# A two-block layer stack on one core: first operands in smaller pieces on two queues, attention states in turn, shifted weight rows in 14 more groups, another last root

## The chip, the cores and the metric

The kernel runs on one core of one Trainium2 chip. The metric is the device time in microseconds; lower is better. The time before is the median of three runs.

## The reference, cut to what matters

All values are float32, one sequence of 256 rows of 1024 (`x`) and 256 memory rows (`mem`). The first block mixes three branches and ends with a feed-forward layer:

```python
h = rms_norm(x, norm_mix)
z = h @ w_in                                   # rnn, q, k, v, g, decay, mq, gates
out_a = rg_lru(causal_dwconv(z_rnn, ...), ...) # linear recurrence over the rows
o_gla = chunked_gla(z_q, z_k, z_v, log_alpha)  # 4 heads, chunks of 64 rows:
#   state = decay * state + k_end.T @ v, one state per chunk and head
out_b = rms_norm(o_gla, gla_norm) * silu(z_g)
mk, mv = split(rms_norm(mem, mem_norm) @ w_mem_kv)
out_c = softmax(mq @ mk.T * scale) @ mv        # 4 heads
x = x + sum(sigmoid(z_gate) * proj(out_a, out_b, out_c)) @ w_out
h2 = rms_norm(x, norm_ffn)
x = x + (gelu(gate) * val) @ w_down            # of causal_dwconv(h2 @ w_up)
x = rms_norm(x, final_norm)
```

The second block has 6 attention heads, a state-space mixer and a pooling mixer side by side, then a SiLU feed-forward layer, and ends with

```python
x = x + (silu(gate) * up) @ w_down_2
return rms_norm(x, norm_final_2)
```

## The kernel before, in words

**Products.** Every long product is made of three matmuls (`mm3`, lines L203 to L205): both operands are split into a high and a low part in a 32-bit format that TensorE reads in one pass, and high x high, high x low and low x high are added in PSUM. `split` (L154) makes the parts: ScalarE copies the high part (L156, or L159 with a gain), VectorE subtracts for the low part (L157, L160). Weights arrive in groups (`memk0`, `v2`, `gate2_0`, `gu5`, ...), each one DMA on SP's queue into a `raw` tile of 1 MB. `emit_half` (L169) splits half a group at a time into a `wh` and a `wl` tile; `load_w` keeps three halves ahead of the half that is used. `chunk_T` (L207) multiplies a group so that features lie on partitions, with the weights as stationary operand and 256 columns; `chunk_tok` (L231) so that rows lie on partitions, with the activations stationary and the weights moving. A half of a usual group is four slices of 256 columns, 24 matmuls. `PLACE` (L73) shifts the `wh` and `wl` tiles of three groups (`up3`, `xbc3`, `gu6`): half 0 begins 28 floats, half 1 begins 30 floats into its buffer.

**Order.** The groups come in the order of `wplan` (L88): `memk`, `memv`, `mq`, `zrnn`, `qk`, `rga`, `rgx`, `v`, `g`, then for the branches 2, 0, 1 four pairs of `gate` and `br`, then `wout`; `up` with `dn` between; the second block's `vz`, `qk2`, `xbc`, `pool`; `wo2`; `gu` with `dn2`. Smaller work (scores, states, transposes, sums) runs on two lanes of generators; `step()` (L404) runs one piece of each lane after a group. `gla_state` (L707) has one piece for each of three chunk states: for the four heads a matmul of 64 rows (L720), rows 0 to 63 for an even chunk and 64 to 127 for an odd one. `gla_scores` comes one step before it, `gla_out` after it, in four further steps, two of them with small products and one with transposes. At each such step TensorE leaves the long products for the small ones; these places are called joints here.

**Start.** ScalarE's queue loads 16 columns of gains (L253). SP's queue loads in turn two memory slices (256 KB, L344) and a quarter of `memk0` and of `memk1` (256 KB each, L363), four times. Thirteen warm-up matmuls (L258) run until then. The sums of squares of the memory rows (`Ssq`, L282 to L297) come after these products; `memk2` follows.

**End.** The last two down products leave 4 banks, two for each half of the rows. For each half (L1333 on) ScalarE squares and sums two banks, VectorE adds, ScalarE takes the root, VectorE takes its reciprocal with one Newton step (L1344 to L1347), and the banks are scaled by it and by the gains `nfb` (`scaled`, L1331). For the second half of the rows the first bank is multiplied by the gains early (L1339) and scaled by ScalarE (L1354); the second bank is scaled by VectorE in two pieces. Tile, the layer that orders the instructions of each engine and makes their waits, may move an instruction within its engine's order.

## Time and profile before

| | |
|---|---|
| median of three runs | 797.58 us (796.61 to 798.03) |
| the profiled execution | 797.59 us, of which span 795.8 us |
| TensorE, busy share of the span | 99% |
| VectorE, ScalarE | 75%, 61% |
| DMA read and written | 141.20 MB, 1.05 MB |
| instructions | 15612 |

The span runs from the first to the last instruction of the program; the rest of the profiled execution's time lies around it. An engine's busy time counts each stretch once in which it has an instruction under way. A matmul record is longer than the distance to the next one, since matmuls are pipelined; so the pace of a stretch is read from the starts, not from the durations. A matmul of two full 32-bit operands leaves two records.

### The profile page before, as it was taken

The page shows a single profiled execution, that of the slowest core. Times are in us where ns is not written, and L with a number is a line of the kernel's source. Part 1 is how long each engine was busy: PE and PEld are TensorE (multiplying, and loading weights), DVE is VectorE, ACT ScalarE, POOL GpSimd, SP SyncE. Part 2 cuts the span into 40 slices and gives each one's busy share as a digit, 9 for nine tenths or more (in the row PEclk, how much of TensorE's full clock was granted, in tenths as well). Part 3 has the DMA queues.
Part 4 walks back from the last instruction along what each step waited for, and adds up shares of the span by engine and source line. Part 5 has one row for each costly group of instructions (what it writes and reads, how often), then busy time and mean ns, then how long its engine had stood idle before and what let it go on. Part 6 is the DMA issues. An engine that isn't in the chain of part 4 may idle for free.

```text
span 795.8 us, 15612 instructions
## 1 busy us (share of the span) xinstructions
PE 785.1 (99%) x6460; PEld 760.9 (96%) x6460; DVE 598.6 (75%) x980; ACT 481.8 (61%) x770; POOL 10.2 (1%) x23
## 2 busy tenths in 40 slices
PE   8999999999999999999999999999999999999996
PEld 8999989999889999999999999999899999999995
DVE  6988757965667777898778887899898756656663
ACT  6845679964345555666556565768976544444443
POOL 0000110000000000000000000000000000000000
PEclk9999999999999999999999999999999999999999
DMA  8864544364445665366555555263174544555521
GB/s 281 305 229 152 175 133 176 114 231 140 144 142 201 203 213 204 110 243 228 171 203 207 173 204 198 103 257 113 49 268 157 215 181 167 203 200 180 205 106 53
DMA packets 23526, 144.03 MB, mean 181 GB/s; under 512 B 2896, under 2 KB 3424, under 8 KB 8480
## 3 DMA queue, kind: packets, MB, share of 16 engines
q1 hardware_dynamic: 22464, 140.98, 49.9%
q0 software_dynamic: 704, 1.80, 0.6%
q8 instruction: 50, 0.82, 0.4%
q10 hardware_dynamic: 288, 0.27, 0.1%
q14 instruction: 20, 0.16, 0.1%
HBM read 141.20 MB, written 1.05 MB: 179 GB/s over the span
## 4 chain that ended last, share of the span: by engine, by line
PE 91%; DVE 4%; ACT 3%; issue 1%; DMA 1%; DVEq 0%; SPq 0%; ACTq 0%
PE ps L203 23%; PE ps L204 22%; PE ps L205 22%; PE aux L203 6%; PE aux L205 6%; PE aux L204 5%; DVE wl L157 2%; PE aux L521 1%; PE ps L220 1%; PE ps L227 1%; PE ps L218 1%; DMA raw<-w 1%; ACT wh L156 1%; PE aux L720 1%; ACT L1154 0%
## 5 line engine op out<-in xcount | busy, mean ns | idle before, releaser
L157 DVE TENSOR_TENSOR wl<-raw,wh 128x1024 fp32r<-128x1024 f32 (+4 forms) x276 | 322.1, 1172 | 119.5 <-ACT wh L156 117.7
L156 ACT ACTIVATE wh<-raw 128x1024 fp32r<-128x1024 f32 (+4 forms) x276 | 277.9, 1015 | 207.2 <-PE ps L204 159.6
L203 PE MATMUL ps<-H,wh 128*128 128x256 f32 x1320 | 368.2, 279 | 1.2 <-ACT wh L156 1.2
L205 PE MATMUL ps<-H,wl 128*128 128x256 f32 x1320 | 366.3, 278 | 0.2 <-DVE wl L157 0.2
L204 PE MATMUL ps<-H,wh 128*128 128x256 f32 x1320 | 366.3, 278 | 0.0
L203 PEld LDWEIGHTS ps<-H,wh 128*128 128x128 f32 x1320 | 248.0, 188 | 3.5 <-issue 1.8
L204 PEld LDWEIGHTS ps<-H,wh 128*128 128x128 f32 x1320 | 248.7, 188 | 0.3
L205 PEld LDWEIGHTS ps<-H,wl 128*128 128x128 f32 x1320 | 248.1, 188 | 0.4 <-DVE wl L157 0.4
L203 PE MATMUL ps<-wh,H 128*128 128x256 f32 (+2 forms) x192 | 54.6, 285 | 0.0
L204 PE MATMUL ps<-wl,H 128*128 128x256 f32 (+2 forms) x192 | 54.0, 281 | 0.3 <-DVE wl L157 0.3
L205 PE MATMUL ps<-wh,H 128*128 128x256 f32 (+2 forms) x192 | 54.1, 282 | 0.0
L205 PE MATMUL aux<-S,wl 128*128 128x256 f32 x192 | 53.1, 277 | 0.0
L204 PE MATMUL aux<-S,wh 128*128 128x256 f32 x192 | 53.1, 276 | 0.0
L203 PE MATMUL aux<-S,wh 128*128 128x256 f32 x192 | 53.1, 276 | 0.0
L156 ACT ACTIVATE S<-t 128x256 fp32r<-128x256 f32 x46 | 19.0, 415 | 50.3 <-DVE t L921 26.5
L543 DVE SCALAR_TENSOR_TENSOR t<-t,par,t 128x255 f32<-128x255 f32 (+1 forms) x96 | 40.1, 478 | 0.1
L204 PEld LDWEIGHTS ps<-wl,H 128*128 128x128 f32 x192 | 36.1, 188 | 0.5 <-DVE wl L157 0.5
L203 PEld LDWEIGHTS ps<-wh,H 128*128 128x128 f32 x192 | 36.1, 188 | 0.4 <-issue 0.4
L205 PEld LDWEIGHTS ps<-wh,H 128*128 128x128 f32 x192 | 36.1, 188 | 0.0
L205 PEld LDWEIGHTS aux<-S,wl 128*128 128x128 f32 x192 | 36.1, 188 | 0.0
L203 PEld LDWEIGHTS aux<-S,wh 128*128 128x128 f32 x192 | 36.1, 188 | 0.0
L204 PEld LDWEIGHTS aux<-S,wh 128*128 128x128 f32 x192 | 36.1, 188 | 0.0
(327 smaller groups left out, 1070.8 us busy)
## 6 DMA issues: line engine op xcount, KB each, us to landing
raw<-w SPq DMA_DIRECT2D x115, 1024.0 KB, 4.8
raw<-w SPq DMA_DIRECT2D x12, 768.0 KB, 4.3
raw<-w SPq DMA_DIRECT2D x12, 256.0 KB, 5.3
raw<-w SPq DMA_DIRECT2D x2, 896.0 KB, 4.5
raw<-w SPq DMA_DIRECT2D x1, 1088.0 KB, 6.2
raw<-w SPq DMA_DIRECT2D x1, 1048.0 KB, 4.8
R<-memT SPq DMA_DIRECT2D x4, 256.0 KB, 5.5
R<-xT SPq DMA_DIRECT2D x2, 512.0 KB, 8.8
```

The source lines that it names most:

```text
L156: act.activation(dst_h, src, AF.Copy)
L157: dve.tensor_tensor(dst_l, src, dst_h.bitcast(F32), op=ALU.subtract)
L203: pe.matmul(o, lh, rh, start=start, stop=False, skip_group_check=skip)
L204: pe.matmul(o, lh, rl, start=False, stop=False, skip_group_check=skip)
L205: pe.matmul(o, ll, rh, start=False, stop=stop, skip_group_check=skip)
L218: pe.matmul(ps[:, m, :], wh[:, k, c], x[0][:, kk, :], start=kk == 0 and m == 0, stop=False, skip_group_check=True)
L220: pe.matmul(ps[:, m, :], wl[:, k, c], x[0][:, kk, :], start=False, stop=False, skip_group_check=True)
L227: pe.matmul(ps[:, m, :], wh[:, k, m * P:(m + 1) * P], x[1][:, kk, :], start=False, stop=kk == nk - 1, skip_group_check=True)
L521: pe.matmul(ps[r0:r1, :], mv[:, mt, hd * DV + d0:hd * DV + d0 + r1 - r0], pts[hd][:, mt, :], start=mt == 0, stop=mt == 1, skip_group_check ...
L543: dve.scalar_tensor_tensor(dst[:, s:], src[:, :S - s], w(width - 1 - s), dst[:, s:], op0=ALU.mult, op1=ALU.add)
L720: pe.matmul(ps[:DK, i, :], kt[r, n // 2, hd * DK:(hd + 1) * DK], gv[r, n // 2, hd * DV:(hd + 1) * DV], start=True, stop=True)
```

## The change

Five edits, named here as the prediction names them.

- **Shifted rows.** `LEAD` names 14 groups. In half 0 of each the first one or two slices begin at the given offset (in floats, within lines of 32), and the further slices at an offset of 0; the class `Rows` does the addressing, and a half is split in two pieces. With `True` as last entry half 0 goes through its slices in the outer loop. `gu3` is added to `PLACE`.
- **Attention states in turn.** Chunks 0 and 1 are made in one step, head by head and chunk by chunk in turn; chunk 2 has the next step, so the steps behind it come one earlier.
- **First operands.** The gains lie ahead of the first memory slice in one transfer of 139 KB; `memk0`'s first quarter comes in two pieces of 128 KB on ScalarE's queue; the second memory slice (128 KB) and `memk1`'s first quarter follow on SP's queue. Ten warm-up matmuls instead of thirteen.
- **Last root.** The root takes the last sum as input and the other sums as bias. Another form of the Newton step, on gains that are doubled once.
- **Scaling from SBUF.** In the second half of the rows both banks are multiplied by the gains before the root is known; ScalarE scales one and VectorE the other, each in one piece.

```diff
@@ -71,9 +71,56 @@
...
-for _n in ("up3", "xbc3", "gu6"):
+for _n in ("up3", "xbc3", "gu6", "gu3"):
...
+LEAD = {
+    "mq1": (28, 30, True),
+    "qk0": (28, 30, True),
+    "gate2_0": (28, 30, True),
+    "gate0_1": (28, 30, True),
+    "gate0_3": (28, 30, True),
+    "memv0": (4, 2, True),
+    "v2": (28, 30, False),
+    "zrnn2": (28, 30, False),
+    "gate2_2": (28, 30, False),
+    "gu2": (28, 30, False),
+    "gate2_3": (28, False),
+    "gate0_0": (30, False),
+    "gate2_1": (4, 2, True),
+    "pool": (4, 2, False),
+}
...
+class Rows:
...
+    def __init__(self, t, b, n, lead):
+        self.t, self.b, self.n = t, b, n
+        self.off, o = [], 0
+        for k in range(n):
+            r = lead[k] if k < len(lead) else 0
+            o += (r - o) % 32
+            self.off.append(o)
+            o += b
+        self.shape = (P, n, b)
+        self.lead = len(lead)
+    def __getitem__(self, i):
+        _, k, c = i
+        a, e, _ = c.indices(self.b)
+        return self.t[:, self.off[k] + a:self.off[k] + e]
...
@@ -180,6 +227,12 @@
...
+        if i == 0 and name in LEAD:
+            hs, ls = (Rows(w, b, a // 2, LEAD[name][:-1]) for w in (wh, wl))
+            for (h, c, r), (l, _, _) in zip(hs.parts(), ls.parts()):
+                split(h, l, raw[:, c].rearrange("p (a b) -> p a b", a=r))
+            loaded[name, i] = (hs, ls)
+            return
...
@@ -209,7 +262,7 @@
...
-            if k_outer:
+            if k_outer or i == 0 and LEAD.get(name, (False,))[-1]:
                 od.sort(key=lambda q: q[1])
...
@@ -249,20 +302,36 @@
...
-    par = cp.tile([P, NPAR], F32, name="par")
-    nc.scalar.dma_start(par[:, :16], ins["par"][:, :16])
...
+    memall = slot("R1", [P, 16 + KT * S])
+    memr = memall[:, 16:].rearrange("p (k s) -> p k s", k=KT)
+    first = ("memk0", "memk1")
+    for n in first:
+        raws[n] = wrp.tile([P, WMAX], F32, tag="raw", name=uid("raw"))
+    def first_w(queue, name, c):
+        o = WOFF[name][0]
+        queue.dma_start(raws[name][:, c], W[o:o + P * 2048].rearrange("(p n) -> p n", p=P)[:, c])
+    nc.sync.dma_start(memall[:, :272], ins["memT"][:, :272])
+    for k in range(2):
+        first_w(nc.scalar, "memk0", slice(256 * k, 256 * k + 256))
+    nc.sync.dma_start(memr[:, 1, :], ins["memT"][:, 272:528])
+    first_w(nc.sync, "memk1", slice(0, 512))
...
-    for _ in range(13):
+    for _ in range(10):
         pe.matmul(wps, ones, ones, start=True, stop=True)
-    memr = slot("R1", [P, KT, S])
...
@@ -340,33 +409,34 @@
...
-    def mem_part(i):
-        nc.sync.dma_start(memr[:, 2 * i:2 * i + 2, :], ins["memT"][:, 2 * i:2 * i + 2, :])
-        for k in (2 * i, 2 * i + 1):
-            split(mh[:, k, :], ml[:, k, :], memr[:, k, :], pv("g_mem", k))
...
     for q in range(4):
-        mem_part(q)
+        ks = (2 * q, 2 * q + 1)
+        if q > 0:
+            nc.sync.dma_start(memr[:, ks[0]:ks[1] + 1, :],
+                              ins["memT"][:, 16 + 512 * q:16 + 512 * q + 512].rearrange("p (a b) -> p a b", a=2))
+            for k in ks:
+                split(mh[:, k, :], ml[:, k, :], memr[:, k, :], pv("g_mem", k))
         for n, name in enumerate(first):
-            if q == 0:
-                raws[name] = wrp.tile([P, WMAX], F32, tag="raw", name=uid("raw"))
...
-            o = WOFF[name][0]
-            cr = slice(512 * q, 512 * q + 512)
-            c = slice(512 * (q % 2), 512 * (q % 2) + 512)
-            nc.sync.dma_start(raws[name][:, cr],
-                              W[o:o + P * 2048].rearrange("(p n) -> p n", p=P)[:, cr])
-            split(fw[n][0][:, c], fw[n][1][:, c], raws[name][:, cr])
+            c0 = 512 * (q % 2)
+            if q > 0:
+                first_w(nc.sync, name, slice(512 * q, 512 * q + 512))
+            if q > 0 or n > 0:
+                split(fw[n][0][:, c0:c0 + 512], fw[n][1][:, c0:c0 + 512], raws[name][:, 512 * q:512 * q + 512])
             for k in range(2):
+                kk = 2 * q + k
+                if q == 0 and n == 0:
+                    c = slice(256 * k, 256 * k + 256)
+                    split(mh[:, kk, :], ml[:, kk, :], memr[:, kk, :], pv("g_mem", kk))
+                    split(fw[n][0][:, c], fw[n][1][:, c], raws[name][:, c])
                 for mo in range(2):
-                    w0 = c.start + k * 256 + mo * P
-                    kk = 2 * q + k
+                    w0 = c0 + k * 256 + mo * P
                     mm3(fps[n][:, mo, :], fw[n][0][:, w0:w0 + P], fw[n][1][:, w0:w0 + P],
                         mh[:, kk, :], ml[:, kk, :], kk == 0 and mo == 0, kk == KT - 1, skip=True)
...
@@ -711,18 +781,21 @@
...
-        for n in range(3):
-            r = slice(64 * (n % 2), 64 * (n % 2) + 64)
+        for ns in ((0, 1), (2,)):
             for hp in range(2):
-                ps = aux([P, 2, DV])
+                pss = [aux([P, 2, DV]) for _ in ns]
                 for i in range(2):
                     hd = 2 * hp + i
-                    pe.matmul(ps[:DK, i, :], kt[r, n // 2, hd * DK:(hd + 1) * DK],
-                              gv[r, n // 2, hd * DV:(hd + 1) * DV], start=True, stop=True)
-                if n == 0:
-                    act.activation(sts[0][:, hp * 384:(hp + 1) * 384],
-                                   ps[:DK].rearrange("p a b -> p (a b)"), AF.Copy)
-                else:
+                    for n, ps in zip(ns, pss):
+                        r = slice(64 * (n % 2), 64 * (n % 2) + 64)
+                        pe.matmul(ps[:DK, i, :], kt[r, n // 2, hd * DK:(hd + 1) * DK],
+                                  gv[r, n // 2, hd * DV:(hd + 1) * DV], start=True, stop=True)
+                for n, ps in zip(ns, pss):
+                    if n == 0:
+                        act.activation(sts[0][:, hp * 384:(hp + 1) * 384],
+                                       ps[:DK].rearrange("p a b -> p (a b)"), AF.Copy)
+                        continue
                     for i in range(2):
                         hd = 2 * hp + i
                         c = slice(hd * DV, (hd + 1) * DV)
...
@@ -1318,46 +1393,55 @@
...
-            for n in range(2):
-                q = slice(n * 512, (n + 1) * 512)
+            for a, q0, nq in RUNS[t]:
+                q = slice(q0, q0 + nq)
                 for k, ((wh, wl), (ph, pl)) in enumerate(zip(ws, phs)):
-                    mm3(accs[2 * t + n], ph[:, c], pl[:, c], wh[:, 0, q], wl[:, 0, q],
+                    mm3(accs[a][:, :nq], ph[:, c], pl[:, c], wh[:, 0, q], wl[:, 0, q],
                         False, k == len(ws) - 1, skip=True)
...
-    def scaled(dst, acc, r, nf):
-        dve.scalar_tensor_tensor(dst, acc, r, nf, op0=ALU.mult, op1=ALU.mult)
+    act.activation(nfb, nfb, AF.Copy, scale=2.0)
...
+    def final(parts, rows, early):
...
+        n = len(parts)
+        ssq, v, u, root = small([P, n]), small([P, n]), small([P, 1]), small([P, 1])
+        o = [t2(), t2()]
+        for i, (a, q0, nq) in enumerate(parts):
+            act.activation(t2()[:, :nq], a[:, :nq], AF.Square, accum_out=ssq[:, i:i + 1])
+            if early:
+                q = q0 % 512
+                dve.tensor_tensor(o[q0 // 512][:, q:q + nq], a[:, :nq], nfb[:, q0:q0 + nq], op=ALU.mult)
+            if i < n - 1:
+                if i == 0:
+                    dve.tensor_scalar(v[:, :1], ssq[:, :1], 1.0 / D, EPS, op0=ALU.mult, op1=ALU.add)
+                else:
+                    dve.scalar_tensor_tensor(v[:, i:i + 1], ssq[:, i:i + 1], 1.0 / D, v[:, i - 1:i],
+                                             op0=ALU.mult, op1=ALU.add)
+        act.activation(root, ssq[:, n - 1:], AF.Sqrt, scale=1.0 / D, bias=v[:, n - 2:n - 1])
+        dve.scalar_tensor_tensor(v[:, n - 1:], ssq[:, n - 1:], 1.0 / D, v[:, n - 2:n - 1],
+                                 op0=ALU.mult, op1=ALU.add)
+        dve.reciprocal(u, root)
+        dve.scalar_tensor_tensor(u, v[:, n - 1:], u, root, op0=ALU.mult, op1=ALU.add)
+        dve.reciprocal(u, u)
+        for h in range(2):
+            c = slice(512 * h, 512 * h + 512)
+            if not early:
+                dve.scalar_tensor_tensor(o[h], parts[h][0], u, nfb[:, c], op0=ALU.mult, op1=ALU.mult)
+                nc.sync.dma_start(out[rows, c], o[h])
+            elif h == 0:
+                act.activation(o[0], o[0], AF.Copy, scale=u)
+                nc.scalar.dma_start(out[rows, c], o[0])
+            else:
+                dve.tensor_scalar(o[1], o[1], u, None, op0=ALU.mult)
+                nc.sync.dma_start(out[rows, c], o[1])
     for t in range(2):
-        ssq = small([P, 2])
-        o = [t2(), t2()]
-        for n in range(2):
-            act.activation(t2(), accs[2 * t + n], AF.Square, accum_out=ssq[:, n:n + 1])
-            if t == 1 and n == 0:
-                dve.tensor_tensor(o[0], accs[2], nfb[:, 0:512], op=ALU.mult)
-        v, r, q = small([P, 1]), small([P, 1]), small([P, 1])
-        dve.tensor_scalar(v, ssq[:, 0:1], 1.0 / D, EPS, op0=ALU.mult, op1=ALU.add)
-        dve.scalar_tensor_tensor(v, ssq[:, 1:2], 1.0 / D, v, op0=ALU.mult, op1=ALU.add)
-        act.activation(r, v, AF.Sqrt)
-        dve.reciprocal(r, r)
-        dve.tensor_tensor(q, r, r, op=ALU.mult)
-        dve.scalar_tensor_tensor(q, q, -0.5, v, op0=ALU.mult, op1=ALU.mult)
-        dve.scalar_tensor_tensor(r, q, 1.5, r, op0=ALU.add, op1=ALU.mult)
-        rows = slice(t * P, (t + 1) * P)
-        if t == 0:
-            for n in range(2):
-                scaled(o[n], accs[n], r, nfb[:, n * 512:(n + 1) * 512])
-                nc.sync.dma_start(out[rows, n * 512:(n + 1) * 512], o[n])
-        else:
-            act.activation(o[0], o[0], AF.Copy, scale=r)
-            nc.scalar.dma_start(out[rows, 0:512], o[0])
-            for i in range(2):
-                c = slice(256 * i, 256 * i + 256)
-                cc = slice(512 + 256 * i, 768 + 256 * i)
-                scaled(o[1][:, c], accs[3][:, c], r, nfb[:, cc])
-                nc.sync.dma_start(out[rows, cc], o[1][:, c])
+        final([(accs[a], q0, nq) for a, q0, nq in RUNS[t]], slice(t * P, (t + 1) * P), t == 1)
...
@@ -1474,7 +1558,7 @@
...
-        "cst2": np.ascontiguousarray(cst2), "xT": tT(g["x"]), "memT": tT(g["mem"]),
+        "cst2": np.ascontiguousarray(cst2), "xT": tT(g["x"]), "memT": np.concatenate([par[:, :16], tT(g["mem"]).reshape(P, KT * S)], axis=1),
```

The edit at `chunk_T` stands in `chunk_tok` too. `RUNS` names for each half of the rows its two banks with first column and width, as they were before.

## Rows read from the trace of the kernel before

**Rows 1.** The cores: span and mean granted TensorE clock.

```profile
core 0: 795.8 us, clock 0.998
```

**Rows 2.** The page: busy time of each engine, and the chain that ended last.

```profile
PE 785.1 (99%) x6460; PEld 760.9 (96%) x6460; DVE 598.6 (75%) x980; ACT 481.8 (61%) x770; POOL 10.2 (1%) x23
PE 91%; DVE 4%; ACT 3%; issue 1%; DMA 1%; DVEq 0%; SPq 0%; ACTq 0%
```

**Rows 3.** Line L203 in four windows: duration min/median/max, first and last start, forms.

```profile
L203 PE MATMUL ps<-H,wh x16: 276/276/277, 669.0 to 674.1; 128*128 128x256 f32 x16
...
L203 PE MATMUL ps<-H,wh x16: 280/282/282, 634.0 to 639.3; 128*128 128x256 f32 x16
...
L203 PE MATMUL ps<-wh,H x40: 279/281/281, 28.2 to 42.0; 128*128 128x256 f32 x40
...
L203 PE MATMUL ps<-wh,H x56: 279/280/281, 133.8 to 153.3; 128*128 128x256 f32 x56
```

**Rows 4.** Line L203 in two windows: the shifted group gu6, then gu7.

```profile
L203 PE MATMUL ps<-H,wh x16: 274/278/284, 646.9 to 652.2; 128*128 128x256 f32 x16
...
L203 PE MATMUL ps<-H,wh x16: 276/276/284, 652.6 to 657.7; 128*128 128x256 f32 x16
```

**Rows 5.** Line L203 in three windows, from gate2_2, gate0_2 and gu4 on.

```profile
L203 PE MATMUL ps<-H,wh x16: 281/282/384, 176.8 to 182.2; 128*128 128x256 f32 x16
...
L203 PE MATMUL ps<-H,wh x24: 280/282/282, 229.9 to 242.2; 128*128 128x256 f32 x24
...
L203 PE MATMUL ps<-H,wh x32: 280/281/282, 628.3 to 639.3; 128*128 128x256 f32 x32
```

**Rows 6.** Timeline of the start: start, length, instruction, count, idle before.

```profile
5.26 0.91 ACT L159 ACTIVATE H<-R,par 128x256 fp32r<-128x256 f32 x2 [2.59 <-DMA par<-par]
...
6.20 0.63 ACT L156 ACTIVATE wh<-raw 128x512 fp32r<-128x512 f32 x1
...
6.88 0.39 PE L203 MATMUL ps<-H,wh 128*128 128x256 f32 x1 [1.18 <-ACT wh L156]
...
7.61 0.39 PE L205 MATMUL ps<-H,wl 128*128 128x256 f32 x1 [0.22 <-DVE wl L157]
```

**Rows 7.** Timeline around the first state step, and of the second block's scores.

```profile
175.09 0.28 PE L205 MATMUL ps<-M,wl 128*128 128x256 f32 x1
175.29 1.54 PE L720 MATMUL aux<-V,S 64*96 64x192 f32 x8
176.76 0.38 PE L203 MATMUL ps<-H,wh 128*128 128x256 f32 x1
...
536.83 0.50 PE L976 MATMUL aux<-M 64*128 64x128 f32 x4
537.16 0.61 PE L977 MATMUL aux<-M 64*128 64x256 f32 x4
```

**Rows 8.** By window: length, busy PE, PEld, DVE, ACT, POOL; then the timeline.

```profile
5.80:7.90 2.10, 0.79 (x4) 0.59 (x5) 1.57 (x3) 2.07 (x5) 0.00 (x0) 1.00 1.05 401
7.90:19.14 11.24, 11.05 (x94) 10.84 (x93) 11.23 (x21) 9.15 (x19) 0.00 (x0) 1.00 0.93 331
...
19.20 0.60 PE L297 MATMUL aux<-ones,t 128*128 128x1 f32 x4 [0.24 <-DVE t L292]
```

**Rows 9.** Timeline of the tail.

```profile
787.53 0.69 DVE L1339 TENSOR_TENSOR t<-aux,GQ 128x512 f32<-128x512 f32 x1 [0.18 <-ACT t L1337]
...
790.05 0.19 ACT L1337 ACTIVATION_READ_ACCUMULATOR t<-aux 128x1 f32 x1
...
790.47 0.20 ACT L1343 ACTIVATE sm<-sm 128x1 f32<-128x1 f32 x1 [0.23 <-DVE sm L1342]
...
791.49 0.72 ACT L1354 ACTIVATE t<-t,sm 128x512 f32<-128x512 f32 x1 [0.81 <-DVE sm L1347]
...
792.00 0.81 SPq L1360 DMA_DIRECT2D out_dram<-t  x2
792.24 0.35 ACTq L1355 DMA_DIRECT2D out_dram<-t  x1
```

More of the change, by code (lines that the diff above doesn't have):

```diff
@@ L73, with parts @@
 PLACE = {}
-for _n in ("up3", "xbc3", "gu6"):
+for _n in ("up3", "xbc3", "gu6", "gu3"):
     PLACE[_n, 0] = 28
     PLACE[_n, 1] = 30
+LEAD = {
[29 more added lines that the diff above has]
+        return self.t[:, self.off[k] + a:self.off[k] + e]
+    def parts(self):
+        b, n, m = self.b, self.n, self.lead
+        d = self.off[m - 1] - self.off[0] if m == 2 else b
+        head = self.t[:, self.off[0]:self.off[0] + m * d].rearrange("p (a b) -> p a b", a=m)[:, :, :b]
+        rest = self.t[:, self.off[m]:self.off[m] + (n - m) * b].rearrange("p (a b) -> p a b", a=n - m)
+        return (head, slice(0, m * b), m), (rest, slice(m * b, n * b), n - m)
 def ffn_plan(up, dn, nf):
@@ L238, in chunk_tok @@
             od = [(t, k) for t in range(2) for k in range(nk // 2)]
-            if k_outer:
+            if k_outer or i == 0 and LEAD.get(name, (False,))[-1]:
                 od.sort(key=lambda q: q[1])
@@ L264, in pv @@
         o, c = POFF[name]
-        return par[:rows, o + i:o + i + n]
+        if o < 16:
+            return memall[:rows, o + i:o + i + n]
+        return par[:rows, o - 16 + i:o - 16 + i + n]
     def cv(name):
@@ L341, in build @@
     m = (mh, ml)
-    def mem_part(i):
-        nc.sync.dma_start(memr[:, 2 * i:2 * i + 2, :], ins["memT"][:, 2 * i:2 * i + 2, :])
-        for k in (2 * i, 2 * i + 1):
-            split(mh[:, k, :], ml[:, k, :], memr[:, k, :], pv("g_mem", k))
-    first = ("memk0", "memk1")
     fps = [bank(), bank()]
@@ L1320, in last_tok @@
             c = slice(t * P, (t + 1) * P)
-            for n in range(2):
-                q = slice(n * 512, (n + 1) * 512)
+            for a, q0, nq in RUNS[t]:
+                q = slice(q0, q0 + nq)
                 for k, ((wh, wl), (ph, pl)) in enumerate(zip(ws, phs)):
-                    mm3(accs[2 * t + n], ph[:, c], pl[:, c], wh[:, 0, q], wl[:, 0, q],
+                    mm3(accs[a][:, :nq], ph[:, c], pl[:, c], wh[:, 0, q], wl[:, 0, q],
                         False, k == len(ws) - 1, skip=True)
```

7 lines of the change are left out of this document (4 added, 3 removed).

## The prediction

> **What bounds the kernel now.** I read the cores first: one core, 795.8 us of span at a granted clock of 0.998 [rows 1], so the clock is not the subject. The page's busy times and its chain of waits come next: TensorE is busy for 99% of the span and makes up 91% of the chain that ended last [rows 2]. So an edit counts if it shortens TensorE's own stream, or the few stretches where TensorE is idle: the first 7 us, a little before 19.2 us, the joints between long products and small ones, and the last 6 us. The other engines' time costs nothing, with one exception found below.
>
> Then I looked at the pace of the long products, one line over short windows: line L203 is the first of the three matmuls of each product, so the distance from its first to its last start, divided by the count less one, is the time of three matmuls. Here is the view that matters most. The same 16 instructions of the same shape take 5.1 us in one place and 5.3 us in another: 340 against 353 ns for three, 113.3 against 117.8 ns for one [rows 3]. Nothing in between persists: each long stretch has one pace from its start to the next joint. Where weights are the moving operand (the token-major products) the slow pace holds too, 13.8 us/39 and 19.5 us/55, that is 354 and 355 ns for three [rows 3]. One matmul at the slow pace costs 4.45 ns more.
>
> **Shifted rows.** The kernel already shifts three groups (up3, xbc3, gu6: all rows of half 0 by 28 floats, of half 1 by 30). Of gu6 the trace shows both sides: gu5 before it is slow [rows 3], gu6 itself takes 5.3 us for 16, and the aligned group behind it 5.1 us [rows 4]. The two other groups behave alike. So a stretch of shifted rows runs at the slow pace itself, and the stream comes out of it at the fast one. The change does this with fewer rows: only the first one or two slices of half 0, at most 12 of a group's 48 matmuls, in 14 groups, and it shifts gu3 whole.
>
> What is slow today behind these places, counted in the code's order: memv0 to memv2 144 matmuls, v2 to g2 192 [rows 3]; gate2_2 with br2_2 84 and, alike, gate0_0 with br0_0 84, gate0_2 to br0_3 168, gu4 and gu5 96 [rows 5], gu2 48, of which I count the second half, 24. Less the 12 shifted ones in each of the first five stretches, 132+180+72+72+156+96+24 = 732 matmuls could change pace: 732 x 4.45 ns = 3.26 us. (gate0_2 has no shift of its own; the state steps move up by one, see below, so no small product stands before it any more and it inherits gate0_1's pace.) On the other side, eight of the 14 groups (mq1, zrnn2, qk0, gate2_0, gate2_1, gate2_3, gate0_1, pool) run fast now but for a few matmuls after the joint; 12 shifted ones cost each up to 53 ns, I take 0.3 us for all eight. That makes -2.96 us if every place works. No row shows so short a shift, none an offset of 4 and 2, and none a shift of the moving operand, which two of the largest places (memv0, v2) need. I take three quarters: -2.45+0.3 = -2.15 us. Bounds: -2.96, and +3.2 from the fourth rival. Each of the 14 halves is split in two pieces, one ScalarE and one VectorE instruction more; the split is issued three halves ahead of its product, so I cost that at nothing. Without that cover it would be at most one further piece a group, 0.63 us on ScalarE [rows 6].
>
> The rule that speaks against this edit: the Trainium skill, page "SBUF — State Buffer", section "Door 1: The DMA port swizzle", says that SBUF is read in lines of 16 bytes and that an access which crosses to a new line pays. Offsets of 28 and 4 floats keep to such lines, 30 and 2 don't. By that rule only the six matmuls at an odd offset would pay, and the eight fast groups would cost 0.15 us instead of 0.3. The trace does not bear it out: gu6 takes 5.3 us over a half at 28 and a half at 30, as much as gu5 without a shift.
>
> **Attention states in turn.** Today the three chunk states are three steps, each between two long products. In the first the last long matmul starts at 175.09, the eight records of L720 at 175.29, and the next long product at 176.76 [rows 7]: 1.67 us for one interruption; the two others take the same time. Each record uses 64 of the 128 rows, and they start one after the other, (1.54-0.32)/7 = 0.174 us apart, 0.32 us being the length of the last. The change puts chunks 0 and 1, which use rows 0 to 63 and 64 to 127, into one step, matmul by matmul in turn, in separate PSUM banks. The attention scores of the second block show what such halves do: L976 and L977 have eight records of two heads, on rows 0 to 63 and 64 to 127, four of 128 columns and four of 256, and they are through 0.94 us after the first start (537.16+0.61-536.83) [rows 7]. One after the other, at L720's 0.174 us for 192 columns, 1536 columns would take 1.39 us. The two streams lie on top of each other. So two states should take the time of one, and one interruption goes: -1.67 us. Bounds: if the halves ran one after the other, only the joint would be saved, 1.67-8 x 0.174 = -0.28 us; at best -1.8 us, the joint's slow start with it. Later steps come one product earlier; their inputs were ready a product earlier as well, and the four aux banks of the step were last used a product before. VectorE gets four more updates in that step, hidden as above.
>
> **First operands.** ScalarE begins at 5.26 us, when the gains land; the first weight piece is there at 6.20, the first real matmul starts at 6.88 and the low part holds TensorE again until 7.61 [rows 6]. With 267 KB instead of 520 KB in front of the first product, the first pair should land near 5.2 us and the first matmul start near 6.1. But VectorE is the exception: from 7.90 to 19.14 us it is busy for 11.23 of 11.24 us, and TensorE's sums at 19.20 wait for its last add [rows 8]. What TensorE gains early it gives back there, unless VectorE's work ends sooner as well. Before 7.90 VectorE has 2.10-1.57 = 0.53 us of idle time [rows 8]; smaller pieces fill part of it, and the two further split instructions that they bring take some back. I take about half, -0.3 us; bounds 0 and, if the gains land 0.35 us sooner as well, -0.8 us. Three warm-up matmuls fewer leave TensorE's idle time before the first product as long as it was.
>
> The Trainium skill, page "DMA: Bandwidth & Descriptors", section "Issuing engines are not separate DMA queues", says that the issuing engines share the same 16 DMA engines and a second one saves only the sequencer's time to issue. By it the second queue is worth an issue, not bandwidth; the order of the bytes has to bring the rest.
>
> **The tail.** Today ScalarE's sum of squares ends at 790.24; then come a VectorE add, the root (790.47 to 790.67), four small VectorE steps of 0.2 us, and scaling from 791.49, with the output transfers issued from 792.00 to 792.81 [rows 9]. With the other sums as bias the root starts 0.2 us sooner, and one step of 0.2 us goes: -0.4 us for the start of scaling. But the last part is now also multiplied by the gains before its root is known, and that product reads the bank that Square reads. The earlier product of this kind waits for its Square (idle until ScalarE's L1337) and takes 0.69 us, the next instruction starting 0.61 us after it [rows 9]. So VectorE is held from 790.27 to 790.88, then come the sum (0.1), reciprocal, combination and reciprocal (0.6): scaling from about 791.59, 0.10 us late. In return one scaling from SBUF replaces two from PSUM, and the last issue is then ScalarE's, at 791.59+0.72+0.03 = 792.34 for 0.35 us, ended at 792.69 instead of 792.81 [rows 9]; the first one is late by about as much. I take +0.05 us; bounds -0.4 and +0.4. Doubling the gains is one ScalarE pass under the last down products; ScalarE is busy for 61% of the span [rows 2], and less there.
>
> **Sum.** Against the profiled execution, 797.59 us (span 795.8 and 1.79 around it; the median of the runs is 797.58): -1.67 -2.15 -0.3 +0.05 = -4.07, so 793.5 us.
>
> **Rivals.**
> First, the short shifts change nothing: the pace after a joint is set by something else. For it: joints come out fast without a shift as well (gu9 has none and is fast). Against it: gu6. Then -1.67-0.3+0.05+0.3 = -1.6: 796.0 us, at the edge of what can be told.
> Second, everything works: -1.67-2.96-0.8-0.4 = -5.8: 791.8 us. It needs the token-major products to take the fast pace.
> Third, the halves of the states don't overlap: -0.28 for -1.67, so 794.9 us. Against it stand L976 and L977.
> Fourth, the other side: shifted rows themselves run at the slow pace [rows 4]; if the stream stays in it, the eight groups that are fast now turn slow with what follows them up to the next joint: mq1 to zrnn1 192, zrnn2 48, qk0 and qk1 96, four gates with their branches 336, pool 48, together 720 x 4.45 ns = 3.2 us. With none of the slow stretches cured: -1.67-0.3+0.05+3.2 = +1.3: 798.9 us. It decides from 1.92 us on, when six in ten of these fall.
>
> **How the numbers follow.** Forecast 52%, first rival 22%, second 12%, third 9%, fourth 5%. The time is that of the likeliest. The range goes from the second rival's to just beyond the first's, 791.6 to 796.3 us. Measured runs of this kernel lie within 0.18%, so 0.2%, 1.6 us, is about what can be told from no change. Faster by more: forecast, second, third and half of the first, 84%; within: the other half of the first and a little of the fourth, 12%; slower: 4%.
>
> **What would show it.** Right: L720 in two steps, the first with 16 records in about the time of eight; 5.1 us for 16 of L203 in 634 to 639, 3.40 us for ten in the mem values' and the g products; L203 near 6.1 us; the sums of the memory rows at about 18.9; L1354's successor near 791.6. Wrong: 5.3 us behind shifted groups, 5.3 us in stretches that are 5.1 now, a wait in front of the second pair of states, or new waits in 505 to 605 us, where ScalarE is nearly full and the order of its table loads could turn out another.

## The result, and the profile after

The changed kernel takes 801.95 us (median of four runs, 801.6 to 802.42) against 797.62 for the kernel before: the ratio is 1.0057, 95% interval 1.0039 to 1.0074. The forecast was 793.5, faster; the time rose by 4.3 us. The profiled execution has a span of 799.8 us, 4.0 more than before [rows 1], and TensorE still is what bounds it.

The cores and the page of the changed kernel, as [rows 1, 2]:

```profile
core 0: 799.8 us, clock 0.997
...
PE 790.4 (99%) x6454; PEld 767.1 (96%) x6454; DVE 599.6 (75%) x993; ACT 483.4 (60%) x786; POOL 10.2 (1%) x23
PE 94%; ACT 3%; DVE 2%; issue 1%; DMA 1%; SPq 0%; ACTq 0%
```

TensorE's busy time rose by 5.3 us with six records fewer, so the loss is pace and not waiting. In the changed kernel the first of the three matmuls of a product is line L256. The same view as [rows 3 to 5], changed kernel, in this order: memv0 half 1 on, v2 half 1 to g2, gate2_2, gu5, gu6, gu7:

```profile
L256 PE MATMUL ps<-wh,H x40: 280/280/281, 27.5 to 41.3; 128*128 128x256 f32 x40
...
L256 PE MATMUL ps<-wh,H x57: 276/279/280, 133.3 to 153.0; 128*128 128x256 f32 x57
...
L256 PE MATMUL ps<-H,wh x16: 276/278/384, 177.0 to 182.3; 128*128 128x256 f32 x16
...
L256 PE MATMUL ps<-H,wh x16: 276/276/277, 638.2 to 643.3; 128*128 128x256 f32 x16
...
L256 PE MATMUL ps<-H,wh x16: 274/278/283, 650.9 to 656.3; 128*128 128x256 f32 x16
...
L256 PE MATMUL ps<-H,wh x16: 276/276/284, 656.6 to 661.7; 128*128 128x256 f32 x16
```

A short way to read it: a duration of 276 or 277 ns goes with the fast pace, 280 or 281 with the slow one. gu5 is cured (5.1 us for 16 instead of 5.3). The two large token-major stretches are not.

The loss stands elsewhere, in a stretch that the prediction never looked at. Line L203 of the kernel before and L256 of the changed one, over up4, the group behind up3:

```profile
L203 PE MATMUL ps<-H,wh x16: 276/277/287, 330.9 to 336.0; 128*128 128x256 f32 x16
```

```profile
L256 PE MATMUL ps<-H,wh x16: 280/281/282, 328.7 to 334.0; 128*128 128x256 f32 x16
```

Here the changed kernel is 2.15 us ahead. Then it runs at 117.8 ns instead of 113.3 from up4 to the last down group of the first feed-forward layer (FFN), 1536 matmuls, and comes out of it 4.66 us behind: 6.81 us lost, and 1536 x 4.45 ns is 6.84. The granted clock reads 1.00 over this stretch in both kernels. xbc0 and qk2_2, the aligned groups behind xbc3, turn slow as well (+0.4, of which +0.25 is left at xbc1). vz1 and its neighbours give back 0.4, gu2 to gu5 0.5, the tail 0.1: 4.66+0.25-0.4-0.5-0.1 = +3.9 of the 4.0 us.

The first operands, as [rows 6, 8]: timeline of the start of the changed kernel, then VectorE's window (length, then busy time of PE, PEld, DVE, ACT, POOL, granted clock, DMA share, GB/s), then the sums of the memory rows:

```profile
4.76 0.51 ACT L206 ACTIVATE H<-R 128x256 fp32r<-128x256 f32 x1 [0.56 <-DMA R<-memT]
...
5.34 0.56 PE L256 MATMUL ps<-H,wh 128*128 128x256 f32 x1
...
6.13 0.41 PE L256 MATMUL ps<-H,wh 128*128 128x256 f32 x1
...
6.34 0.42 PE L257 MATMUL ps<-H,wh 128*128 128x256 f32 x1
...
7.90:18.50 10.60, 10.15 (x89) 9.96 (x87) 10.25 (x20) 8.96 (x19) 0.00 (x0) 1.00 0.95 344
...
18.84 0.61 PE L366 MATMUL aux<-ones,t 128*128 128x1 f32 x4 [0.79 <-DVE t L361]
```

The first product starts 1.54 us sooner, VectorE is busy for 10.25 of the 10.60 us from 7.90 on, and TensorE waits 0.8 us for its last add, as the prediction's working has it; 0.7 us of the lead is left behind memk2.

The states, as [rows 7]: sixteen records now take the 1.54 us that eight took, and the next product starts 1.47 us after their first:

```profile
175.49 1.54 PE L792 MATMUL aux<-V,S 64*96 64x192 f32 x16
176.96 0.38 PE L256 MATMUL ps<-H,wh 128*128 128x256 f32 x1
```

The tail, as [rows 9]:

```profile
794.05 0.19 ACT L1415 ACTIVATION_READ_ACCUMULATOR t<-aux 128x1 f32 x1
794.28 0.29 ACT L1425 ACTIVATE sm<-sm,sm 128x1 f32<-128x1 f32 x1
794.28 0.69 DVE L1418 TENSOR_TENSOR t<-aux,GQ 128x512 f32<-128x512 f32 x1 [2.00 <-ACT t L1415]
...
795.60 0.72 ACT L1437 ACTIVATE t<-t,sm 128x512 f32<-128x512 f32 x1 [1.02 <-DVE sm L1430]
...
796.11 0.33 SPq L1441 DMA_DIRECT2D out_dram<-t  x1
796.35 0.35 ACTq L1438 DMA_DIRECT2D out_dram<-t  x1
```

The product with the gains waits for its own Square. Scaling starts 1.36 us after the sum of squares (794.24 to 795.60; before 1.25), and the last issue ends 2.46 us after it (796.70; before 2.57). Both are within 0.02 us of the prediction's working.

### The profile page after: what moved, and what is told of

Its sections match the earlier page's. It is cut to its first block, busy times and chain, and to the rows that moved or that the text cites. A ratio compares the mean times of both kernels' runs of the same rounds, so it can differ in the third digit from the quotient of the medians.

```text
span 799.8 us, 15628 instructions
## 1 busy us (share of the span) xinstructions
PE 790.4 (99%) x6454; PEld 767.1 (96%) x6454; DVE 599.6 (75%) x993; ACT 483.4 (60%) x786; POOL 10.2 (1%) x23
## 4 chain that ended last, share of the span: by engine, by line
PE 94%; ACT 3%; DVE 2%; issue 1%; DMA 1%; SPq 0%; ACTq 0%
PE ps L256 23%; PE ps L257 23%; PE ps L258 23%; PE aux L256 6%; PE aux L257 6%; PE aux L258 6%; PE aux L591 1%; PE ps L273 1%; PE ps L271 1%; PE ps L280 1%; ACT wh L203 1%; DMA R<-memT 1%; DVE wl L204 1%; PE aux L821 0%; PE aux L827 0%
## 5 line engine op out<-in xcount | busy, mean ns | idle before, releaser
L203 ACT ACTIVATE wh<-raw 128x1024 fp32r<-128x1024 f32 (+4 forms) x291 | 279.5, 972 | 213.5 <-PE ps L257 169.0
L256 PE MATMUL ps<-H,wh 128*128 128x256 f32 x1320 | 369.4, 280 | 0.0
L256 PEld LDWEIGHTS ps<-H,wh 128*128 128x128 f32 x1320 | 249.7, 189 | 1.9 <-issue 1.6
L256 PE MATMUL ps<-wh,H 128*128 128x256 f32 (+2 forms) x192 | 54.5, 284 | 0.0
L256 PE MATMUL aux<-S,wh 128*128 128x256 f32 x192 | 54.0, 281 | 0.0
L257 PE MATMUL aux<-S,wh 128*128 128x256 f32 x192 | 54.0, 281 | 0.0
L203 ACT ACTIVATE S<-t 128x256 fp32r<-128x256 f32 x46 | 19.0, 416 | 50.0 <-DVE t L994 26.2
L256 PEld LDWEIGHTS aux<-S,wh 128*128 128x128 f32 x192 | 36.9, 192 | 0.0
L256 PEld LDWEIGHTS ps<-wh,H 128*128 128x128 f32 x192 | 36.1, 188 | 0.4 <-issue 0.4
```

The source lines that it names most:

```text
L203: act.activation(dst_h, src, AF.Copy)
L256: pe.matmul(o, lh, rh, start=start, stop=False, skip_group_check=skip)
L257: pe.matmul(o, lh, rl, start=False, stop=False, skip_group_check=skip)
```

## The experiments

Times are medians; each group of runs stands beside runs of the kernel before on the same chip, 797.3 to 797.8 us, and the ratio is to them. Pace by stretch comes from each run's trace.

### One edit at a time

**Shifts alone.** The kernel before with LEAD, Rows and gu3 in PLACE:

```diff
-for _n in ("up3", "xbc3", "gu6"):
+for _n in ("up3", "xbc3", "gu6", "gu3"):
...
+        if i == 0 and name in LEAD:
```

> The kernel before with the shifted rows alone (the 14 groups of LEAD and gu3 in PLACE). Open is what turned the first FFN, from up4 to its last down group, from the fast pace (113.3 ns a matmul) to the slow one (117.8), which is worth 6.8 us. If the pace behind up3 hangs on how the stream arrives there and any edit ahead of it can flip it, this run may come out either way: about 797.1 with the first FFN fast (the groups of LEAD ahead of it together lose some 0.3 us, gu2 to gu5 win 0.9), about 804 with it slow. If the place of the constants (64 bytes lower in the changed kernel) decides, the first FFN stays fast here, since this kernel leaves them where they were: 797.1.

798.18 us, ratio 1.0009 (0.9999 to 1.0018). The first FFN stays fast, so the shifts don't cause the loss. Nor do they bring the 2.15 us. L256 of this run from the middle of mq2 through zrnn0, and over gate2_0; then L203 of the kernel before over the same two:

```profile
L256 PE MATMUL ps<-H,wh x23: 281/281/281, 57.1 to 64.8; 128*128 128x256 f32 x23
...
L256 PE MATMUL ps<-H,wh x16: 279/280/283, 154.6 to 159.9; 128*128 128x256 f32 x16
```

```profile
L203 PE MATMUL ps<-H,wh x24: 276/276/277, 56.9 to 64.7; 128*128 128x256 f32 x24
...
L203 PE MATMUL ps<-H,wh x16: 276/276/283, 153.6 to 158.7; 128*128 128x256 f32 x16
```

Two groups that were fast come out slow: mq1 with what follows up to zrnn1 (0.8 us) and gate2_0 with br2_0 (0.4). That the shift alone does it is not shown for mq1: mq2 to zrnn1 are fast in the profile of the changed kernel, which has the same shift, and slow in a kernel without it (the one below with the constants at 87808). zrnn2 and qk0 pay for a slow half (0.1 us each), gate2_1, gate2_3, gate0_1 and pool for some of one. memv0, v2, gate0_0 and gate0_3 change nothing. gate2_2 with br2_2 is cured (0.26), and gu2 to gu5 (0.5); the products of vz1 wait 0.4 us less.

**States alone.** 

> The kernel before with the attention states in turn alone. The step took 1.6 us off the changed kernel up to the first FFN: 796.0 if the first FFN stays at the fast pace, about 802.8 if this edit alone flips up4 and what follows to the slow one. By the place of the constants, which is unchanged here, it stays fast.

```diff
-        for n in range(3):
-            r = slice(64 * (n % 2), 64 * (n % 2) + 64)
+        for ns in ((0, 1), (2,)):
...
+                    for n, ps in zip(ns, pss):
+                        r = slice(64 * (n % 2), 64 * (n % 2) + 64)
```

795.46 us, ratio 0.9974 (0.9963 to 0.9984): 2.1 us faster, and the first FFN stays fast. The step of 16 records, gate0_2, gate0_3 and the first matmul of gate1_0 in this run, then that matmul in the kernel before:

```profile
175.29 1.54 PE L722 MATMUL aux<-V,S 64*96 64x192 f32 x16
...
L203 PE MATMUL ps<-H,wh x16: 276/276/276, 225.4 to 230.5; 128*128 128x256 f32 x16
...
L203 PE MATMUL ps<-H,wh x16: 276/276/369, 236.1 to 241.3; 128*128 128x256 f32 x16
...
245.74 0.28 PE L203 MATMUL ps<-H,wh 128*128 128x256 f32 x1
```

```profile
248.05 0.37 PE L203 MATMUL ps<-H,wh 128*128 128x256 f32 x1
```

2.31 us are gained by gate1_0, and 2.40 by the end of that group, which no longer starts behind a joint. Of these 0.75 are pace: gate0_2 and br0_2 now follow fast products without a joint ahead and keep their pace, and gate0_3 and br0_3, now behind a joint, come out of it fast; both pairs were slow before [rows 5], and 168 x 4.45 ns is 0.75. The rest, 1.65, is the interruption.

**First operands alone.** 

> The kernel before with the first operands in pieces on two queues alone (10 warm-up matmuls in place of 13, the first 16 parameters in front of the memory, par 16 columns shorter, so that the constants and R1 lie 64 bytes lower). In the changed kernel the stream was 0.74 us ahead from the first memv group on: 796.9 if the first FFN stays fast, 803.7 if it turns slow. By the place of the constants it turns slow here and in no other of these four but the next.

```diff
-    for _ in range(13):
+    for _ in range(10):
...
-    par = cp.tile([P, NPAR], F32, name="par")
+    par = cp.tile([P, NPAR - 16], F32, name="par")
+    memall = slot("R1", [P, 16 + KT * S])
```

803.26 us, ratio 1.0074 (1.0059 to 1.0089). The loss is in this edit, and it is the first FFN that turns slow (L203, up4 of this run):

```profile
L203 PE MATMUL ps<-H,wh x16: 280/281/281, 329.5 to 334.8; 128*128 128x256 f32 x16
```

### What in the first operands does it

Three things changed at once: three warm-up matmuls fewer, where the stream stands in time, and addresses. par is 16 columns shorter and R1's slot 16 columns longer, so that the constants (cst) lie at byte 88064 of each partition instead of 88128, and R1 at 89600 instead of 89664; all else keeps its place.

**Warm-ups alone (13 to 10).** 

> The kernel before with one number changed: 10 warm-up matmuls in place of 13, which is what the first-operands edit does to TensorE's own list of instructions. The first-operands edit alone turned up4 to the last down group slow. If the cause is the number of TensorE's instructions ahead (everything behind sits three matmuls earlier in its list), that comes back here: the first FFN slow, about 804. If the cause is where the stream stands in time, or the addresses, 797.6 and the first FFN at 113.3 ns a matmul.

798.24 us, ratio 1.0007 (0.9998 to 1.0017), the first FFN fast. Not the warm-ups.

**The changed kernel with 13 warm-ups.** 

> The changed kernel with 13 warm-up matmuls as before, its one change. By the number of TensorE's instructions the first FFN and xbc0 to qk2_2 go back to the fast pace: 801.9 less 7.2 is 794.7. By the addresses or the time of the stream they stay slow: 801.9, or some tenths less, since the first memk group would find the granted clock at its upper level.

802.75 us, ratio 1.0069 (1.0054 to 1.0084): the first FFN is still slow, and mq1 to zrnn1 turned slow as well.

**Addresses alone.** 

> The kernel before with the addresses of the changed one and nothing else: the first 16 parameters stand in front of the memory in R1's slot, par is 16 columns shorter, so that constants and R1 begin 64 bytes lower; the transfers, their order and the 13 warm-ups are those of before. By the addresses the first FFN turns slow: 804.4. By the other two reasons 797.6.

```diff
-    par = cp.tile([P, NPAR], F32, name="par")
-    nc.scalar.dma_start(par[:, :16], ins["par"][:, :16])
+    par = cp.tile([P, NPAR - 16], F32, name="par")
+    memall = slot("R1", [P, 16 + KT * S])
+    memr = memall[:, 16:].rearrange("p (k s) -> p k s", k=KT)
+    nc.scalar.dma_start(memall[:, :16], ins["par"][:, :16])
```

804.44 us, ratio 1.009 (1.0075 to 1.0105), the forecast of this theory to 0.1 us. Behind mq0 only two stretches change their pace: up4 to the last down group and xbc0 to qk2_2, the two behind the shifted groups up3 and xbc3 (L203, up4):

```profile
L203 PE MATMUL ps<-H,wh x16: 280/281/281, 330.8 to 336.1; 128*128 128x256 f32 x16
```

**The constants moved the other way.** 

> The kernel before with one change of place: the tile of constants is allocated ahead of the parameters, so that it begins at a multiple of 128 bytes as in the changed kernel and not 64 past one; every other operand of a matmul keeps its address and no instruction changes. If that place decides the pace behind the norm's matmuls on the constants (which stand right ahead of up3 and xbc3), the first FFN turns slow: 804.8. If it doesn't, 797.6 and every group at its old pace.

```diff
+    cst = cp.tile([P, NCST], F32, name="cst")
     par = cp.tile([P, NPAR], F32, name="par")
...
-    cst = cp.tile([P, NCST], F32, name="cst")
```

797.59 us, ratio 1.000 (0.9991 to 1.001). With the constants at 86656 nothing changed. I had taken the remainder at 128 for the one that counts; that form of the theory fell here.

**The constants 64 bytes lower, R1 where it was.** 

> The kernel before with the tile of constants exactly 64 bytes lower, at the address of the changed kernel, and R1 where it was (the first 16 parameters take the 64 bytes between them as a tile of their own). The addresses alone turned the first FFN slow; what moved in them was the constants, R1 and the parameters. The two matmuls right ahead of up3 and of xbc3 read the constants, and R1 isn't touched between 309 and 331 us. If the constants' address is the cause, the first FFN turns slow: 804.4. If R1's is, 797.6.

```diff
-    par = cp.tile([P, NPAR], F32, name="par")
-    nc.scalar.dma_start(par[:, :16], ins["par"][:, :16])
+    par = cp.tile([P, NPAR - 16], F32, name="par")
     warm = cp.tile([P, 1], F32, name="warm")
+    cst = cp.tile([P, NCST], F32, name="cst")
+    par0 = cp.tile([P, 16], F32, name="par0")
+    nc.scalar.dma_start(par0, ins["par"][:, :16])
...
-    cst = cp.tile([P, NCST], F32, name="cst")
```

804.24 us, ratio 1.0095 (1.0078 to 1.0112). The constants' address it is. Where the two kernels part can be seen at the joint ahead of up3: TensorE's last work before it is two matmuls on the constants, which spread the norm's factors. (up2, ahead of the joint, is slow in every run here, so the pace at which the stream arrives is not what differs.) Kernel before, then changed kernel, the starts from there on:

```profile
324.96 0.38 PE L327 MATMUL aux<-cst,sm 128*128 128x128 f32 x2
325.10 0.37 PE L203 MATMUL ps<-H,wh 128*128 128x256 f32 x1
325.30 0.28 PE L204 MATMUL ps<-H,wh 128*128 128x256 f32 x1
325.42 0.28 PE L205 MATMUL ps<-H,wl 128*128 128x256 f32 x1
```

```profile
322.81 0.38 PE L396 MATMUL aux<-cst,sm 128*128 128x128 f32 x2
322.94 0.37 PE L256 MATMUL ps<-H,wh 128*128 128x256 f32 x1
323.15 0.29 PE L257 MATMUL ps<-H,wh 128*128 128x256 f32 x1
323.27 0.28 PE L258 MATMUL ps<-H,wl 128*128 128x256 f32 x1
```

The second and third matmuls of up3 start 120 ns apart in the one and 125 in the other. From there the shifted groups run through different series of spacings (start to start, ns: 205, 120, 116, 117, 120, 119, 117 against 205, 125, 117, 118, 120, 117, 117), and one leads out at the fast pace, the other does not. xbc3 shows the same two series.

**Four more places for the constants.** Ones narrower, the warm-ups on ones in x's slot, and padding, so that cst moves alone among the operands (the widths of the padding are those for 87808):

```diff
-    ones = cp.tile([P, P], F32, name="ones")
+    ones = cp.tile([P, 1], F32, name="ones")
...
+    cp.tile([P, 40], F32, name="pad0")
+    cst = cp.tile([P, NCST], F32, name="cst")
+    cp.tile([P, 80], F32, name="pad1")
```

> The kernel before with the constants at byte 87808 of a partition (a multiple of 256) and every other operand of a weight matmul where it was; the tile of ones is one column wide, the warm-ups read ones written into the slot of x, and the rest is padding. Known are 88128 and 86656 with the first FFN fast, 88064 with it slow. 88064 is a multiple of 256 and the two others are not: by a rule of multiples of 256 (or of 256 in the distance to something fixed) this one is slow, 804.3. By a rule of multiples of 512 or more, or if the slow place is a single one, it is fast, 797.6.

> As the run above with the constants at 87936, an odd multiple of 128 as 86656 is. By multiples of 256 fast, 797.6; it would be slow, 804.3, only if lower places near 88064 are slow whatever their remainder.

> As the run above with the constants at 88000, which leaves 192 over a multiple of 256, and 64 over one of 128 as 88128 does. By multiples of 256 or of 128 fast, 797.6; slow, 804.3, if nearness to 88064 counts.

> As the run above with the constants at 87872, which is 256 below 88128 and leaves the same 64 over a multiple of 256. By multiples of 256 fast, 797.6, as 88128. Slow, 804.3, would rule out any rule that goes by the remainder at 256.

One execution each: 804.41 us at 87808, and 796.77, 796.45 and 797.75 at the three others (before 797.81). L203 over up4, one fence for each kernel in this order:

```profile
L203 PE MATMUL ps<-H,wh x16: 280/281/281, 330.7 to 336.0; 128*128 128x256 f32 x16
```

```profile
L203 PE MATMUL ps<-H,wh x16: 276/276/286, 330.0 to 335.1; 128*128 128x256 f32 x16
```

```profile
L203 PE MATMUL ps<-H,wh x16: 276/276/286, 329.7 to 334.8; 128*128 128x256 f32 x16
```

```profile
L203 PE MATMUL ps<-H,wh x16: 276/276/286, 331.2 to 336.3; 128*128 128x256 f32 x16
```

Of seven places, the two at a multiple of 256 bytes (88064, 87808) are slow and the five others fast. (The 1.0 us between the fast ones stands ahead of up3 and has another cause; see v1 to gate0_3 in the last section.)

### The shift is needed as well

> The kernel before with up3 taken out of PLACE, so that its rows stand where every other group's do. If the shift is what lets the stream leave up3 at the fast pace, the first FFN stays slow to its end, at 117.8 ns: 797.6 plus 6.8 is 804.4. If the shift has nothing to do with it, 797.6.

```diff
-for _n in ("up3", "xbc3", "gu6"):
+for _n in ("xbc3", "gu6"):
```

804.45 us, ratio 1.0088 (1.0073 to 1.0103): without the shift the first FFN is slow with the constants at 88128 too, and xbc0, behind the shift that is left, is fast. So up3's shift does what the prediction says of gu6's, but only together with a place of the constants.

### The loss taken out

**The changed kernel, constants ahead of the parameters (at 86656).** 

> The changed kernel with the constants allocated ahead of the parameters, so that they lie where the run of the kernel before with moved constants had them, with its first FFN fast; R1 stays 64 bytes lower. If the constants' address is the cause, the first FFN and xbc0 to qk2_2 go back to 113.3 ns: 801.9 less 7.2 is 794.7. If R1's is, 801.9.

```diff
     dve.memset(ones, 1.0)
+    cst = cp.tile([P, NCST], F32, name="cst")
     par = cp.tile([P, NPAR - 16], F32, name="par")
...
-    cst = cp.tile([P, NCST], F32, name="cst")
```

794.84 us, ratio 0.9972 (0.9961 to 0.9983), 7.1 us under the changed kernel for one line moved (L256, up4):

```profile
L256 PE MATMUL ps<-H,wh x16: 276/276/286, 329.4 to 334.5; 128*128 128x256 f32 x16
```

**The same with gu2 alone in LEAD.** 

> The last kernel with gu2 alone left in LEAD (gu3 stays in PLACE): states in turn, first operands, tail, and the shifts of the second FFN that worked. If the constants' address is the cause and the shifts ahead of the second FFN are worth little or less than nothing, as the run with the shifts alone says: 797.6 less 2.1 (states), 0.7 (start), 0.8 (gu2 to gu5) and 0.1 (tail) is 793.9, at or under the run above. If the shifts pay together with the rest, it is above the run above by their worth.

794.45 us, ratio 0.9968 (0.9957 to 0.998).

**The same with seven groups in LEAD.** 

> The changed kernel with the constants ahead of the parameters (at 86656) and seven of its 14 shifted groups left: gate2_1, gate2_2, gate2_3, gate0_1, gate0_3, pool and gu2, behind which the stream ran faster in the run with all of them. Their sums of spacing there against the run with gu2 alone are 0.3 (gate2_1), 0.3 (gate2_3), 0.3 (gate0_1), 0.4 (gate0_2) and 0.5 us (vz1), and v2 to g2 stood 0.8 us better in the run without a shift in v2: 794.4 less 1.8 is 792.7 if all of these hold together. If the pace of v1 to g2 is a matter of the single execution and not of the shift in v2, 793.4; if the groups answer to one another, anywhere up to 794.8.

794.33 us, ratio 0.9961 (0.9947 to 0.9975), the lowest median, but no further than gu2 alone brings. The 1.8 us did not add up: v1 to g2 came out slow this time with no shift near, pool's second half and xbc1 too.

**The seven groups on the old start.** 

> The same seven shifted groups, gu3, the states in turn and the new tail on the kernel before, with the first operands, the 13 warm-ups and all addresses as before (constants at 88128). Against the run above it shows what the first operands in pieces are worth when the first FFN is fast in both: the run with all edits and the constants moved was 0.5 us ahead when it entered memk2's second half, the changed kernel 0.7 behind the first memv group, so this one is expected 0.5 to 0.8 us above the run above; if the half-clock first matmuls and the wait for VectorE eat all of it, the two are equal.

794.69 us, ratio 0.9963 (0.9948 to 0.9977). The first operands are worth 0.4 us in the medians, which is no more than the scatter of these runs; in the two profiled spans it is 0.9 (791.9 against 792.8).

## Why the prediction was wrong

**The step that failed** is "So a stretch of shifted rows runs at the slow pace itself, and the stream comes out of it at the fast one", with "The two other groups behave alike" for its proof. It was read off gu6 and held to be a property of the shift. For up3 and xbc3 it hangs on the constants' address too, which the two matmuls ahead of them read. The first operands move that address by 64 bytes, and the prediction priced those by transfers and VectorE only: bounds 0 and -0.8, where the edit alone measured +5.7 us. The one term that decided the sign was in no rival. The fourth rival has the right mechanism (the stream stays in the slow pace behind a shifted group), but counts the 720 matmuls behind groups that the change touches; the 1536 behind up3, which it leaves alone, were not asked about.

**Shifted rows, -2.15.** Wrong by themselves too: +0.6 us alone, inside the bounds (-2.96 to +3.2) and on the other side of zero. Of the stretches counted as slow, gate2_2 and gu2 to gu5 took the fast pace; memv0 to memv2, v2 to g2 and gate0_0 did not. Of the eight fast groups, mq1 and gate2_0 lost theirs (gate2_0 in the changed kernel too, mq1 not). What the shift of two slices does can't be read from a shift of a whole group.

**States, -1.67.** The mechanism held to the record, 16 in the time of eight, and so did the size: 1.65 us for the interruption. The 0.75 more came from gate0_2 to br0_3. That gate0_2 inherits the pace of gate0_1 the prediction foresaw, but booked under the shifts; it takes none. It is luck in part: where v1 is fast (the run with gu2 alone in LEAD), gate0_2 and br0_2 inherit the slow pace of gate0_1 instead, and from v1 to gate1_0 the states gain 1.2 us, not 2.3.

**First operands, -0.3.** The mechanism held (VectorE full, the sums at 18.84 where 18.9 was forecast), though the first product came at 5.34 where 6.1 was forecast; the size is -0.4 by the last pair of runs, not clear of their scatter. What was left out is the address.

**Tail, +0.05.** The working held to 0.02 us; the span's end says -0.06.

With the address put right and everything else as in the change, 794.84 us against the forecast of 793.5: the states gave more by the pace behind them, the shifts next to nothing.

## What to carry to other kernels

When an edit changes the size of a tile, list which tiles behind it in the allocation move and which long streams read them or start behind a matmul that reads them; a free edit of 64 bytes cost 7 us here. Where a trace shows two paces for one and the same instruction, look at where the pace changes: here mostly at a joint or behind shifted rows. Ask of each long stretch what its joint reads, where that lies and how fast the stretch ahead runs, and try two or three addresses early. A cure seen at one place (gu6) is a row about that place.

## What the runs showed of the hardware

**A long stream of equal matmuls has two steady paces**, 113.3 and 117.8 ns, and keeps the one that it has once taken over 1536 of them. For up4 on it is decided within the first group behind a joint. With the constants at a multiple of 256 bytes up3 and xbc3 lead to the slow one, at five other places to the fast one. It is no law for all joints: gu3, with the same shift and the same kind of joint, leads to the fast pace in the changed kernel, whose constants are at 88064. But there the group ahead of the joint is fast as well, since gu2 is shifted too, and ahead of up3 it is slow; no run separates the two. L256 of the changed kernel, the end of up2, then the end of gu2:

```profile
L256 PE MATMUL ps<-H,wh x9: 281/281/281, 319.6 to 322.5; 128*128 128x256 f32 x9
...
L256 PE MATMUL ps<-H,wh x8: 276/276/280, 624.2 to 626.5; 128*128 128x256 f32 x8
```

Why 256, and how a read that is over can act on the reads behind it, no run here shows. The Trainium skill, page "SBUF — State Buffer", section "Door 1: The DMA port swizzle", counts in lines of 16 bytes; all seven places are multiples of 16, so that rule doesn't tell them apart.

**Other stretches took either pace with nothing changed ahead of them, and their paces hang together.** v2 to g2 run slow in the kernel before [rows 3] and fast in the profiled execution with up3 plain, which is the same program up to up3, and gate2_0 the other way round. L203 of that run, v2 half 1 on:

```profile
L203 PE MATMUL ps<-wh,H x17: 276/276/276, 133.7 to 139.2; 128*128 128x256 f32 x17
```

From v1 to gate0_3 it makes 1.06 us in this run (0.19 behind the kernel before at v1, 0.87 ahead at up4), most of the width of the runs of the kernel before (796.5 to 797.9), and more than several of the edits here are worth. Eleven of the profiled kernels have no edit in that stretch, and they show just two chains. In five, the kernel before among them, v1 to g2 are slow, gate2_0 and gate2_1 fast, gate2_2 slow, gate2_3 fast, gate0_0 slow, gate0_1 fast, gate0_2 and gate0_3 slow, and gate1_0 starts 125.00 us behind v1. In the six others each of these is the other way round, and it is 123.94 us. Here are gate2_0 and gate2_2 of the run with up3 plain (in the kernel before gate2_0 is fast, as shown with the shifts alone, and gate2_2 slow [rows 5]):

```profile
L203 PE MATMUL ps<-H,wh x16: 281/281/283, 152.8 to 158.1; 128*128 128x256 f32 x16
...
L203 PE MATMUL ps<-H,wh x16: 276/276/385, 176.6 to 181.8; 128*128 128x256 f32 x16
```

So the pace of a stretch goes with that of the stretches ahead of it, and not with its joint alone. Nor does a change of pace take a joint: the first matmul of gate2_0 follows the last of g2 by 0.12 us, only the roles of the operands change, and the two have different paces in both chains. The prediction's "one pace from its start to the next joint" does not hold there. What picks the chain at v1 no run here shows.

**Ten warm-ups can be too few.** With 10 in place of 13 and the old start, the granted clock of the first real matmuls was 0.59 on the mean, between the two levels of 1.2 and 2.4 GHz; before it was 1.00 over the same stretch, after 13 warm-ups (length, busy times, granted clock third from the end):

```profile
6.90:9.90 3.00, 2.75 (x12) 2.55 (x13) 2.65 (x5) 3.00 (x7) 0.00 (x0) 0.59 1.01 365
```

It is one execution: the clock fell to 0.50, the lower level, at 7.43 us and rose again at 10.84, after 1.97 us without a matmul (1.18 in the kernel before, where it stayed up), and the stream is 0.66 us behind at v1. In the changed kernel the first matmuls are 0.21 us apart (6.13 to 6.34 above), nearly twice the later spacing, though the granted clock of that stretch reads 1.00. The trace has no record of the clock there: its first is a rise to the upper level at 7.20 us (4.20 in the kernel before), the view takes time without a record as 1.00, and from 7.20 on the matmuls are 0.12 us apart. So these products ran at the lower level. It changes little in the end: with the first operands alone the rise came at 4.47 us, and the lead behind memk2 is 0.66 us there against 0.74.
